# Mixer output projection: both groups normed before the product, summed in one PSUM bank

## The chip, the core and the metric

The kernel runs on one core of a Trainium2 chip. The metric is device time in microseconds of one execution. TensorE does the products, VectorE (DVE) and ScalarE (ACT) everything between them, SyncE (SP) issues the loads of weights.

## The reference, cut to what matters

Two transformer blocks on 512 tokens of width 1024, in fp32. The change touches the end of the first block's mixer and the start of its feed-forward part:

```python
a = mla(...)                      # 8 heads, 512 wide
c = short_gated_conv(...)         # 512 wide
m = jnp.concatenate([rmsnorm(a, attn_group_norm[i]),
                     rmsnorm(c, conv_group_norm[i])], axis=-1)
x = x + rmsnorm(m @ w_out[i], mix_post_norm[i])
h = rmsnorm(x, ffn_pre_norm[i])
...
e = rmsnorm(p[i] @ w_ple_proj[i], ple_norm[i])
```

Both group norms are over the 512 channels of a token, so their factor is one number per token. It can be applied to the operand of `m @ w_out` or to that group's product.

## The kernel before, in words

Activations lie channels by tokens, in tiles of 128 x 512. Every fp32 operand is split into a high and a low part (`split`: a copy on ACT, a subtraction on DVE), and a product of two 128-deep tiles is three matmuls (`mm3`, L170 to L172): this is called a unit here. Weights come as 128 x 1024 tiles through SP and are split as well (L131 on ACT, L115 on DVE), from three buffers each.

TensorE executes in the order in which the program is written (the schedule of that engine is manual, L82); ACT, DVE and SP are ordered by a planner that works from priorities and estimated times. The order on TensorE is written with Python generators that yield after each unit: `pull(gen, n)` puts n units at this place, `drain(gen)` the rest. `attention` (L557) runs eight heads; between a head's steps it pulls units from a fill, `per(h)` for head h, and `PER[2]` before the last head's product with the values.

A norm (`Norm`) has four steps. `square` adds up squares on ACT and DVE. `column` (L394) transposes the sums on TensorE and starts `root`, some ten small DVE instructions on one column, at raised priority. `spread` (L432) transposes the column back over 128 partitions on TensorE, and ACT copies the result to a tile `rb`. Then a tile is scaled with it (`apply_norm`, L148, DVE). `first()` queues what DVE is given meanwhile behind the root.

Before the change the group norms act on the products. `conv_out` (L824) multiplies the gated convolution's tiles, with only the gain applied (`split_gain`), by `w_oc`; each of 8 output tiles is scaled by `n_conv.r` on its way out of its bank into `ys`. `out_unit` (L893) does the same for the attention with `w_oa`: DVE scales the bank by `n_att.r` (L109), adds it to `ys` (L112), ACT squares the sum and DVE adds the square up for the norm that follows, `n_post`. The last three output tiles are done in two halves of 256 tokens, so that the first half's norm can start while the second half runs. `boundary` (L938) then goes on with the first half: its root beside units of the fill (`embed`, the projection of the layer's extra embedding), its spread, the residual sum, and the feed-forward part's first products, half by half.

The fill of the attention (`mixer_fill`, L836) holds, in this order: the projections of heads 1 to 6 and what is left of `w_in` (61 units in six shares), then the splits of the four convolution tiles, the projection of head 7, two of eight `embed` tiles, and `conv_out` with the column and the spread of its norm between its units. After the attention come six more units, the column of the attention's norm, the rest of the fill and four of the attention's units, then the spread.

Of the kernel before, what the change touches and what calls it, by code (L numbers as in the profile page):

```python
# [14 lines left out]
P = 128  # L15
T = 512
NT = T // P
D = 1024
KT = D // P
# [17 lines left out]
N_RET = (14, 6)  # L37
# [26 lines left out]
def kernel(  # L64
# [32 lines left out]
    def f32(ap):  # L97
        return ap.bitcast(F32)
# [31 lines left out]
    def copy(out, a):  # L130
        act.activation(out, a, AF.Copy)  # L131
# [37 lines left out]
    def mm3(out, ah, al, bh, bl, start, stop):  # L169
        pe.matmul(out, lhsT=ah, rhs=bh, start=start, stop=False)  # L170
        pe.matmul(out, lhsT=al, rhs=bh, start=False, stop=False)  # L171
        pe.matmul(out, lhsT=ah, rhs=bl, start=False, stop=stop)  # L172

    ALL = slice(0, T)
    HALVES = (slice(0, T // 2), slice(T // 2, T))

    def units(out, w, cols, acts, start=True, stop=True, tok=ALL):
        hi, lo = w  # L180
        n = len(acts)
        for i, (c, a) in enumerate(zip(cols, acts)):
            mm3(out[:, tok], hi[:, c:c + P], lo[:, c:c + P], a[:, 0, tok], a[:, 1, tok],
                start and i == 0, stop and i == n - 1)
            if i < n - 1:
                yield

    def load4(src, n, acts=None, prepare=None, start=0, pool=None):
# [429 lines left out]
    def embed(n):  # L618
        for mt in range(len(es), len(es) + n):
            if mt % 2 == 0:  # L620
                w = weights(w_ple_proj[(mt // 4) * P:(mt // 4 + 1) * P, mt % 4 * 2 * P:(mt % 4 + 2) * 2 * P], 4 * P)
            ps = bank()
            yield from units(ps, w, K8[:2] if mt % 2 == 0 else K8[2:4], pp)
            y = f32(es_t[mt // 2][:, mt % 2, :])
            with tc.high_priority(offset=HE):
                copy(y, ps)
            es.append(y)
            if mt >= 6:
                n_e.square(y)
            yield  # L630
# [4 lines left out]
    with tc.tile_pool(name="m1", bufs=1) as m1, tc.tile_pool(name="pt1", bufs=1) as ptp:  # L635
# [5 lines left out]
        hn = []  # L641
# [153 lines left out]
        qs = {}  # L795
        n_att, heads = Norm(512), []

        def split_head(i):
            heads.append(split_gain(att[i], g_("attn_gn", i)))
# [24 lines left out]
        def conv_out():  # L824

            for mt in range(KT):
                if mt % 2 == 0:
                    w = weights(rows(w_oc, mt // 2))
                    ys_t.append(pair())
                ps = bank()  # L830
                yield from units(ps, w, K8[mt % 2 * 4:mt % 2 * 4 + 4], mixed)
                ys.append(f32(ys_t[-1][:, mt % 2, :]))
                n_conv.then(lambda y=ys[-1], ps=ps: mul(y, ps, n_conv.r))
                yield

        def mixer_fill():  # L836
            for h in range(1, 7):
                yield from project(h)
                if h == 6:
                    embed_load()  # L840
                for _ in range(left * h // 6 - left * (h - 1) // 6):
                    next(fill, None)
                    yield
            yield from fill
            es_t.append(pair())
# [12 lines left out]
            n_conv.spread()  # L858
            yield from co

        def mla_head(h):
            def done(po):
                join(att[h // 2][64 * (h % 2):64 * (h % 2) + 64, :], po)
                if h % 2:
                    n_att.square(att[h // 2])
                    if h == 7:
                        split_head(3)
# [10 lines left out]
        for f in late:  # L878
# [1 line left out]
        pull(fill, LAT[5])  # L880
        left = 13 * KT - sum(LAT[:6])
        mf = mixer_fill()
        per = [left * (h + 1) // 6 - left * h // 6 + 2 + h % 2 * 2 for h in range(6)]
        attention(8, mla_head, mf, lambda h: per[h] if h < 6 else PER[h - 6], ptp, PER[2], urgent=True,
                  at_last=lambda: [split_head(i) for i in range(3)])
        pull(mf, OUT[0])
        n_att.column()
        with n_att.first():
            drain(mf)

        def out_unit(mt, ps, w, tok):  # L893
            yield from units(ps, w, K8[mt % 2 * 4:mt % 2 * 4 + 4], heads, tok=tok)

            def evacuate():
                y, t = ys[mt][:, tok], tmp()[:, tok]
                mul(t, ps[:, tok], n_att.r[:, tok])
                add(y, y, t)
                (n_post if tok == ALL else n_post.halves[HALVES.index(tok)]).square(y)  # L900
            n_att.then(evacuate)
            yield

        def att_out():
            for mt in range(5):
                if mt % 2 == 0:
                    w = weights(rows(w_oa, mt // 2))
                yield from out_unit(mt, bank(), w, ALL)

            ws = [w] + [weights(rows(w_oa, 3))] * 2  # L910
            ps3 = [bank() for _ in ws]
            n_post.fold()
            for tok in HALVES:
                for k in range(3):
                    yield from out_unit(5 + k, ps3[k], ws[k], tok)
# [40 lines left out]
        return banks, units4(banks, src, acts, loaded=loaded, tok=b.tok)  # L956


    es_t += [pair(), pair()]
# [616 lines left out]
```

## Time and profile before

| | |
|---|---|
| median of 3 runs | 1975.17 us (1974.32 to 1975.25) |
| profiled execution | 1974.2 us, its span 1972.5 us |
| TensorE busy | 1948.5 us, 99% of the span |
| DVE busy | 1289.7 us, 65% |
| ACT busy | 914.4 us, 46% |
| mean granted clock of TensorE | 0.996 of full |
| stretch of the change | about 140 to 252 us of the span |

The table is a sum over stages of different kinds. TensorE is busy nearly all the time, so what a change in one stage is worth shows in the few places where TensorE waits, and in the granted clock there.

### The profile page before, as it was taken

To read this page: it belongs to the slowest core of one execution; us is meant where nothing else is said; L and a number is where in the kernel's file an instruction comes from. 1 tells how busy PE (TensorE), PEld (TensorE's weight loads), DVE (VectorE), ACT (ScalarE), POOL (GpSimd) and SP (SyncE) were. 2 spreads that over 40 slices of the span, in tenths; PEclk is the share of its full clock that TensorE was granted. 3 is DMA by queue.
4 is the path that set the end of the run, shared out by engine and by line. 5 is a ranking of instruction groups with operands and counts; after the bars stand their busy time and mean duration, and the time that the engine had idled before them with its cause. 6 is when DMAs were issued, how large, how long until landed. Compare 5 with 4: busy or idle time off the path is not lost.

```text
span 1972.5 us, 26036 instructions
## 1 busy us (share of the span) xinstructions
PE 1948.5 (99%) x10212; PEld 1668.0 (85%) x10212; DVE 1289.7 (65%) x2322; ACT 914.4 (46%) x1557; POOL 9.7 (0%) x21
## 2 busy tenths in 40 slices
PE   9999999999999999999999999999999999999998
PEld 7787888888888888888888898898888888889897
DVE  7878963343459764636467575675598987667575
ACT  5776542232235444324445353444476755344352
POOL 1000000000000000000000000000000000000000
PEclk9999999999999999999999999999999999999999
DMA  5122223333232322232223332323322233332321
GB/s 186 65 65 91 86 85 96 97 97 96 91 118 75 108 80 80 97 96 75 75 92 103 105 97 96 118 86 99 91 88 83 74 102 107 97 116 88 118 75 65
DMA packets 59050, 185.44 MB, mean 94 GB/s; under 512 B 6928, under 2 KB 10400, under 8 KB 58928
## 3 DMA queue, kind: packets, MB, share of 16 engines
q1 hardware_dynamic: 53936, 176.02, 28.0%
q10 hardware_dynamic: 4688, 7.40, 1.2%
q8 instruction: 80, 1.31, 0.3%
q0 software_dynamic: 304, 0.36, 0.1%
q14 instruction: 42, 0.34, 0.1%
HBM read 181.56 MB, written 2.20 MB: 93 GB/s over the span
## 4 chain that ended last, share of the span: by engine, by line
PE 82%; DVE 10%; ACT 4%; DMA 2%; issue 2%; SPq 0%; POOLq 0%; POOL 0%; ACTq 0%; DVEq 0%
PE bank L172 25%; PE bank L170 25%; PE bank L171 24%; PE bank L311 6%; DVE pair L115 2%; DVE wl L115 2%; DMA qr<-in_m_w_dram 1%; ACT pair L131 1%; DVE tmp L112 1%; PE bank L532 1%; ACT wh L131 1%; PE bank L513 1%; ACT tmp L500 1%; DVE pt L115 1%; DVE tmp L1094 1%
## 5 line engine op out<-in xcount | busy, mean ns | idle before, releaser
L170 PE MATMUL bank<-pair,wh 128*128 128x512 f32 (+1 forms) x2166 | 829.7, 383 | 0.3 <-ACT pair L131 0.3
L172 PE MATMUL bank<-pair,wh 128*128 128x512 f32 (+1 forms) x2166 | 820.7, 379 | 0.5 <-DVE pair L115 0.3
L171 PE MATMUL bank<-pair,wl 128*128 128x512 f32 (+1 forms) x2166 | 819.3, 378 | 0.1
L131 ACT ACTIVATE wh<-wr 128x1024 fp32r<-128x1024 f32 (+5 forms) x331 | 326.1, 989 | 667.4 <-PE bank L172 404.2
L115 DVE TENSOR_TENSOR wl<-wr,wh 128x1024 fp32r<-128x1024 f32 (+5 forms) x331 | 375.7, 1138 | 159.5 <-ACT wh L131 158.5
L172 PEld LDWEIGHTS bank<-pair,wh 128*128 128x128 f32 x2166 | 408.0, 188 | 78.4 <-DVE pair L115 1.7
L171 PEld LDWEIGHTS bank<-pair,wl 128*128 128x128 f32 x2166 | 408.5, 189 | 72.4 <-DVE wl L115 0.9
L170 PEld LDWEIGHTS bank<-pair,wh 128*128 128x128 f32 x2166 | 408.5, 189 | 72.4 <-ACT pair L131 0.9
L131 ACT ACTIVATE pair<-tmp 128x512 fp32r<-128x512 f32 (+1 forms) x236 | 146.0, 627 | 86.2 <-DVE tmp L1313 25.9
L112 DVE TENSOR_TENSOR x<-x,bank 128x512 f32<-128x512 f32 (+1 forms) x99 | 66.0, 669 | 176.5 <-PE bank L172 176.4
L115 DVE TENSOR_TENSOR pair<-tmp,pair 128x512 fp32r<-128x512 f32 (+1 forms) x204 | 137.6, 686 | 17.7 <-ACT pair L131 16.0
L311 PE MATMUL bank<-q,pair 128*128 128x256 f32 x1152 | 146.3, 282 | 1.2 <-DVE bank L112 1.1
L311 PEld LDWEIGHTS bank<-q,pair 128*128 128x128 f32 x1152 | 140.7, 189 | 3.7 <-DVE bank L112 3.7
L109 DVE TENSOR_TENSOR tmp<-bank,rb 128x512 f32<-128x512 f32 (+1 forms) x76 | 50.2, 666 | 103.9 <-PE bank L172 101.6
L1095 ACT ACTIVATE tmp<-tmp 128x512 f32<-128x512 f32 x64 | 40.2, 629 | 89.0 <-DVE tmp L1094 89.0
L170 PE MATMUL bank<-wh,pair 128*128 128x512 f32 x200 | 79.3, 396 | 0.6 <-ACT tmp L131 0.6
L172 PE MATMUL bank<-wl,pair 128*128 128x512 f32 x200 | 78.0, 390 | 0.0
L171 PE MATMUL bank<-wh,pair 128*128 128x512 f32 x200 | 77.9, 389 | 0.0
L311 PE MATMUL bank<-pair,wh 128*128 128x256 f32 x384 | 76.3, 282 | 0.0
L500 ACT ACTIVATE tmp<-tmp,small 128x512 f32<-128x512 f32 (+1 forms) x96 | 53.4, 557 | 33.4 <-DVE small L497 32.2
L112 DVE TENSOR_TENSOR tmp<-tmp 128x512 f32<-128x512 f32 (+1 forms) x90 | 56.8, 632 | 14.0 <-ACT tmp L385 13.4
L311 PEld LDWEIGHTS bank<-pair,wh 128*128 128x128 f32 x384 | 62.5, 189 | 0.2
(182 smaller groups left out, 1846.4 us busy)
## 6 DMA issues: line engine op xcount, KB each, us to landing
wr<-in_m_w_dram SPq DMA_DIRECT2D x104, 512.0 KB, 3.7
wr<-in_r_qkg_dram SPq DMA_DIRECT2D x32, 512.0 KB, 3.5
qr<-in_m_w_dram SPq DMA_DIRECT2D x24, 512.0 KB, 3.7
wr<-in_w_gate_dram SPq DMA_DIRECT2D x20, 512.0 KB, 3.5
wr<-in_w_up_dram SPq DMA_DIRECT2D x20, 512.0 KB, 3.5
wr<-in_w_down_dram SPq DMA_DIRECT2D x16, 512.0 KB, 3.4
wr<-in_r_v_dram SPq DMA_DIRECT2D x16, 512.0 KB, 3.5
wr<-in_r_out_dram SPq DMA_DIRECT2D x16, 512.0 KB, 3.7
```

The source lines that it names most:

```text
L109: dve.tensor_tensor(out=out, in0=a, in1=b, op=ALU.mult)
L112: dve.tensor_tensor(out=out, in0=a, in1=b, op=ALU.add)
L115: return dve.tensor_tensor(out=out, in0=a, in1=b, op=ALU.subtract)
L131: act.activation(out, a, AF.Copy)
L170: pe.matmul(out, lhsT=ah, rhs=bh, start=start, stop=False)
L171: pe.matmul(out, lhsT=al, rhs=bh, start=False, stop=False)
L172: pe.matmul(out, lhsT=ah, rhs=bl, start=False, stop=stop)
L311: pe.matmul(out, lhsT=x[:, c], rhs=y, start=start and k + i == 0, stop=k == 3 and i == 2, skip_group_check=True)
L500: act.activation(s[:, :n], s[:, :n], AF.Exp, bias=self.mx[:, col], scale=-1.0, accum_out=self.sm[:, col])
L513: pe.transpose(pt[:, j * P:(j + 1) * P], s[:, j * P:(j + 1) * P], ident)
L532: pe.matmul(o, lhsT=a, rhs=b, start=j == 0 and a is v, stop=j == NT - 1 and a is v)
L1095: act.activation(t, t, AF.Square)
```

## The change

Both groups are normed before their products: `normed` applies the factor and the gain on DVE and splits the result. The convolution's products then stay in their banks (`out_ps`) and the attention's products add up on top of them (`start=False`). A bank is copied out by ACT and squared from the bank by ACT (`evacuate`). The first three output tiles are done row by row of the operand (`by_rows`), for the convolution and for the attention, so that one normed tile serves three banks. Seven banks are held from the convolution's products on; the eighth output tile's convolution products are done in halves just ahead of its attention products. The norm of the convolution gets its column and its spread between four `embed` tiles; the shares of the fill are spread over seven heads and not six.

```diff
-W_OUT = (8, 3, 5, 13, 13)
+W_OUT = (8, 2, 2, 13, 13)
-PER = (14, 10, 6)
-OUT = (6, 6)
+PER = (10, 6)
+OUT = 6
-CO = (4, 11)
+CO = (4, 4)
+    def by_rows(outs, ws, cols, acts, start):
+        for k, a in enumerate(acts):
+            for out, w, c in zip(outs, ws, cols):
+                c = slice(c + k * P, c + k * P + P)
+                mm3(out, w[0][:, c], w[1][:, c], a[:, 0, :], a[:, 1, :], start and k == 0,
+                    k == len(acts) - 1, True)
+                yield
+        def normed(norm, src, gname, i):
+            t, pr = tmp(), pair()
+            apply_norm(t, src, g_(gname, i), norm.r)
+            split(pr, t)
+            return pr
         def conv_out():
-            for mt in range(KT):
...
-                n_conv.then(lambda y=ys[-1], ps=ps: mul(y, ps, n_conv.r))
+            ws = [weights(rows(w_oc, i)) for i in range(2)]
+            out_ps.extend(bank() for _ in range(3))
+            yield from by_rows(out_ps, (ws[0], ws[0], ws[1]), (0, T, 0), mixed, True)
+            for mt in range(3, 7):
...
         def mixer_fill():
-            for h in range(1, 7):
+            for h in range(1, 8):
...
-            for c in range(4):
-                mixed.append(split_gain(conv[c], g_("conv_gn", c)))
-            yield from project(7)
-            yield from embed(2)
-            co = conv_out()
+            em = embed(4)
             for _ in range(CO[0]):
-                next(co)
+                next(em)
                 yield
             n_conv.column()
             for _ in range(CO[1]):
-                next(co)
+                next(em, None)
                 yield
             n_conv.spread()
-            yield from co
+            for c in range(4):
+                mixed.append(normed(n_conv, conv[c], "conv_gn", c))
+            yield from em
+            yield from conv_out()
...
-        pull(mf, OUT[0])
+        pull(mf, OUT)
         n_att.column()
         with n_att.first():
             drain(mf)
+        n_att.spread()
+        for i in range(4):
+            heads.append(normed(n_att, att[i], "attn_gn", i))
+        def evacuate(mt, tok):
...
+            copy(ys[mt][:, tok], out_ps[mt][:, tok])
+            (n_post if tok == ALL else n_post.halves[HALVES.index(tok)]).square(out_ps[mt][:, tok])
         def att_out():
+            ws = [weights(rows(w_oa, i)) for i in range(2)]
+            yield from by_rows(out_ps[:3], (ws[0], ws[0], ws[1]), (0, T, 0), heads, False)
+            for mt in range(3):
+                evacuate(mt, ALL)
...
         out = att_out()
-        with n_att.first():
-            pull(out, OUT[1])
-        n_att.spread()
-        pull(out, 32 + W_OUT[0] - OUT[1])
+        pull(out, 36 + W_OUT[0])
         n_post.halves[0].column()
...
-    banks, rest = boundary(n_post, ys, "mix_post", ffn_in, embed(4), W_OUT, w_gu, hn, w4)
+    banks, rest = boundary(n_post, ys, "mix_post", ffn_in, embed(2), W_OUT, w_gu, hn, w4)
```

## Rows read from the trace of the kernel before

**Rows 1.** The page, busy time by engine: us, share of the span, instructions.
```profile
PE 1948.5 (99%) x10212; PEld 1668.0 (85%) x10212; DVE 1289.7 (65%) x2322; ACT 914.4 (46%) x1557; POOL 9.7 (0%) x21
```
**Rows 2.** Waits of TensorE, 140 to 340 us: us in total, times, longest.
```profile
PE bank L398 <- DVE tmp L112: 3.3, 2, 2.3
...
PE bank L435 <- DVE small L423: 0.8, 1, 0.8
```
**Rows 3.** Timeline, last heads: start, us, engine line, xcount [idle before <-releaser].
```profile
152.27 0.63 ACT L131 ACTIVATE pair<-tmp 128x512 fp32r<-128x512 f32 x1 [0.61 <-DMA tmp<-in_pT_dram]
...
153.40 0.51 PE L532 MATMUL bank<-pt,pair 128*128 128x512 f32 x1 [0.90 <-ACT pt L131]
...
154.44 1.20 PE L532 MATMUL bank<-pt,pair 128*64 128x512 f32 x7 [0.54 <-DVE pt L115]
...
168.98 0.62 PE L513 MATMUL bank<-ident,tmp 128*128 128x128 f32 x3 [1.56 <-ACT tmp L504]
```
**Rows 4.** Windows: busy PE, PEld, DVE, ACT, POOL, granted clock, DMA share, GB/s.
```profile
152.00:156.00 4.00, 2.57 (x13) 1.78 (x12) 4.00 (x9) 3.73 (x8) 0.00 (x0) 0.97 0.35 113
156.00:160.00 4.00, 4.00 (x15) 3.40 (x15) 3.12 (x7) 3.86 (x8) 0.00 (x0) 0.61 0.07 23
168.00:172.00 4.00, 3.02 (x15) 2.54 (x16) 3.71 (x16) 1.77 (x5) 0.00 (x0) 1.00 0.25 63
214.00:218.00 4.00, 1.66 (x11) 1.47 (x10) 3.85 (x12) 0.84 (x2) 0.00 (x0) 0.90 0.67 207
218.00:222.00 4.00, 4.00 (x17) 3.25 (x16) 2.78 (x12) 2.05 (x4) 0.00 (x0) 0.68 0.15 57
```
**Rows 5.** Windows by stage: head 6 with its neighbours, and the attention's output products.
```profile
153.00:169.00 16.00, 13.51 (x62) 10.85 (x62) 14.33 (x35) 14.30 (x30) 0.00 (x0) 0.89 0.31 99
197.00:217.00 20.00, 17.66 (x110) 15.78 (x109) 17.65 (x33) 9.29 (x17) 0.00 (x0) 1.00 0.32 109
```
**Rows 6.** Timeline from the attention norm's column to the first half's column.
```profile
190.81 0.66 PE L398 MATMUL bank<-ident,tmp 128*128 128x128 f32 x4
...
195.71 0.16 DVE L423 SCALAR_TENSOR_TENSOR small<-small 128x4 f32<-128x4 f32 x1
...
196.77 0.60 PE L435 MATMUL bank<-ident,small 128*128 128x128 f32 x4
...
197.13 0.48 PE L170 MATMUL bank<-pair,wh 128*128 128x512 f32 x1
...
199.96 0.39 PE L170 MATMUL bank<-pair,wh 128*128 128x512 f32 x1
...
200.64 0.39 PE L170 MATMUL bank<-pair,wh 128*128 128x512 f32 x1
...
212.95 0.28 PE L170 MATMUL bank<-pair,wh 128*128 128x256 f32 x1
...
213.31 0.28 PE L170 MATMUL bank<-pair,wh 128*128 128x256 f32 x1
...
216.53 0.44 PE L398 MATMUL bank<-ident,tmp 128*128 128x128 f32 x2 [2.34 <-DVE tmp L112]
```
**Rows 7.** Timeline of the latents' norm: its spread, and the first tile's split.
```profile
51.22 1.09 PE L435 MATMUL bank<-ident,small 128*128 128x128 f32 x8 [0.74 <-DVE small L423]
...
53.32 0.63 ACT L131 ACTIVATE pair<-tmp 128x512 fp32r<-128x512 f32 x1 [0.33 <-DVE tmp L148]
...
54.53 0.69 DVE L115 TENSOR_TENSOR pair<-tmp,pair 128x512 fp32r<-128x512 f32 x1
```
**Rows 8.** Timeline of the convolution's norm: its column and the end of its root.
```profile
163.27 0.60 PE L398 MATMUL bank<-ident,tmp 128*128 128x128 f32 x4
...
171.95 0.15 DVE L109 TENSOR_TENSOR small<-small 128x4 f32<-128x4 f32 x1
```
**Rows 9.** Groups by shape, 197 to 217 us: xcount, busy, mean ns, idle before.
```profile
L109 DVE TENSOR_TENSOR tmp<-bank,rb 128x512 f32<-128x512 f32 x5 | 3.4, 688 | 2.3 <-ACT rb L131 1.6 <-PE bank L172 0.7
```
**Rows 10.** Timeline: ACT copies an embedding tile out of its bank.
```profile
221.38 0.60 ACT L131 ACTIVATE pair<-bank 128x512 f32<-128x512 f32 x1 [0.60 <-PE bank L172]
```

More of the change, by code (lines that the diff above doesn't have):

```diff
@@ L167, in rows, with mm3, units @@
         return src[mt * P:(mt + 1) * P, k0 * P:(k0 + nk) * P]
[L169 to L172, printed above, removed]
+    def mm3(out, ah, al, bh, bl, start, stop, loose=False):
+        pe.matmul(out, lhsT=ah, rhs=bh, start=start, stop=False, skip_group_check=loose)
+        pe.matmul(out, lhsT=al, rhs=bh, start=False, stop=False, skip_group_check=loose)
+        pe.matmul(out, lhsT=ah, rhs=bl, start=False, stop=stop, skip_group_check=loose)
     ALL = slice(0, T)
     HALVES = (slice(0, T // 2), slice(T // 2, T))
-    def units(out, w, cols, acts, start=True, stop=True, tok=ALL):
+    def units(out, w, cols, acts, start=True, stop=True, tok=ALL, loose=False):
         hi, lo = w
@@ L183, in units @@
             mm3(out[:, tok], hi[:, c:c + P], lo[:, c:c + P], a[:, 0, tok], a[:, 1, tok],
-                start and i == 0, stop and i == n - 1)
+                start and i == 0, stop and i == n - 1, loose)
             if i < n - 1:
+                yield
[5 more added lines that the diff above has]
+                    k == len(acts) - 1, True)
                 yield
@@ L796 @@
         n_att, heads = Norm(512), []
-        def split_head(i):
-            heads.append(split_gain(att[i], g_("attn_gn", i)))
         def project(h):
@@ L822, in project @@
             yield
-        def conv_out():
-            for mt in range(KT):
[L827 to L832, printed above, removed]
-                n_conv.then(lambda y=ys[-1], ps=ps: mul(y, ps, n_conv.r))
+        def normed(norm, src, gname, i):
[3 more added lines that the diff above has]
+            return pr
+        out_ps = []
+        def conv_out():
+            ws = [weights(rows(w_oc, i)) for i in range(2)]
+            out_ps.extend(bank() for _ in range(3))
+            yield from by_rows(out_ps, (ws[0], ws[0], ws[1]), (0, T, 0), mixed, True)
+            for mt in range(3, 7):
+                if mt == 3:
+                    w = ws[1]
+                elif mt % 2 == 0:
+                    w = weights(rows(w_oc, mt // 2), 8 * P if mt < 6 else 4 * P)
+                out_ps.append(bank())
+                yield from units(out_ps[-1], w, K8[mt % 2 * 4:mt % 2 * 4 + 4], mixed, loose=True)
                 yield
         def mixer_fill():
-            for h in range(1, 7):
+            for h in range(1, 8):
                 yield from project(h)
@@ L840, in mixer_fill @@
                     embed_load()
-                for _ in range(left * h // 6 - left * (h - 1) // 6):
+                for _ in range(left * h // 7 - left * (h - 1) // 7):
                     next(fill, None)
@@ L844, in mixer_fill @@
             yield from fill
-            es_t.append(pair())
-            for c in range(4):
-                mixed.append(split_gain(conv[c], g_("conv_gn", c)))
-            yield from project(7)
-            yield from embed(2)
-            co = conv_out()
+            es_t.extend(pair() for _ in range(2))
+            em = embed(4)
             for _ in range(CO[0]):
-                next(co)
+                next(em)
                 yield
@@ L882 @@
         mf = mixer_fill()
-        per = [left * (h + 1) // 6 - left * h // 6 + 2 + h % 2 * 2 for h in range(6)]
-        attention(8, mla_head, mf, lambda h: per[h] if h < 6 else PER[h - 6], ptp, PER[2], urgent=True,
-                  at_last=lambda: [split_head(i) for i in range(3)])
-        pull(mf, OUT[0])
+        per = [left * (h + 1) // 7 - left * h // 7 + 2 + h % 2 * 2 for h in range(7)] + [PER[0]]
+        attention(8, mla_head, mf, lambda h: per[h], ptp, PER[1], urgent=True)
+        pull(mf, OUT)
         n_att.column()
@@ L889 @@
             drain(mf)
[L893 to L902, printed above, removed]
-        def att_out():
[L905 to L908, printed above, removed]
+        n_att.spread()
@@ new lines @@
+        for i in range(4):
+            heads.append(normed(n_att, att[i], "attn_gn", i))
+        def evacuate(mt, tok):
+            if len(ys) == mt:
+                if mt % 2 == 0:
+                    ys_t.append(pair())
+                ys.append(f32(ys_t[-1][:, mt % 2, :]))
+            copy(ys[mt][:, tok], out_ps[mt][:, tok])
+            (n_post if tok == ALL else n_post.halves[HALVES.index(tok)]).square(out_ps[mt][:, tok])
+        def att_out():
+            ws = [weights(rows(w_oa, i)) for i in range(2)]
+            yield from by_rows(out_ps[:3], (ws[0], ws[0], ws[1]), (0, T, 0), heads, False)
+            for mt in range(3):
+                evacuate(mt, ALL)
+            w = ws[1]
+            for mt in (3, 4):
+                if mt == 4:
+                    w = weights(rows(w_oa, 2))
+                yield from units(out_ps[mt], w, K8[mt % 2 * 4:mt % 2 * 4 + 4], heads, start=False, loose=True)
+                evacuate(mt, ALL)
+                yield
@@ L910, in att_out @@
             ws = [w] + [weights(rows(w_oa, 3))] * 2
-            ps3 = [bank() for _ in ws]
+            last = weights(w_oc[3 * P:4 * P, 4 * P:8 * P], 4 * P)
+            out_ps.append(bank())
             n_post.fold()
             for tok in HALVES:
-                for k in range(3):
-                    yield from out_unit(5 + k, ps3[k], ws[k], tok)
+                for mt in (5, 6, 7):
+                    c = K8[mt % 2 * 4:mt % 2 * 4 + 4]
+                    if mt == 7:
+                        yield from units(out_ps[mt], last, K8[:4], mixed, tok=tok, loose=True)
+                        yield
+                    yield from units(out_ps[mt], ws[mt - 5], c, heads, start=False, tok=tok, loose=True)
+                    evacuate(mt, tok)
+                    yield
@@ L956, in boundary @@
         return banks, units4(banks, src, acts, loaded=loaded, tok=b.tok)
-    es_t += [pair(), pair()]
+    es_t.append(pair())
     hn = [pair() for _ in range(KT)]
```

2 lines of the change are left out of this document (removed).

## The prediction

> **What bounds the kernel now.** I read the page first: TensorE is busy 99% of the span, DVE 65% [rows 1]. Only two things can move the time: how much TensorE has to do, and where it waits or runs slow. So next come the waits of TensorE in the stretch of the change, 140 to 340 us. The reader is to see that they are few: 3.3 us in two transposes of norm sums, one of them 2.3, and 0.8 for a spread [rows 2]; the timeline of the last heads adds 0.90 and 0.54 before a product with the values and 1.56 before a transpose [rows 3]. Third, the granted clock around each. After the 0.90 and 0.54 the mean clock is 0.97 and then 0.61 of two windows of 4 us; after the 2.34 it is 0.90 and 0.68; after the 1.56 it stays 1.00 [rows 3, 4, 6]. The missing clock is (0.03 + 0.39) x 4 = 1.68 us and (0.10 + 0.32) x 4 = 1.68 us: TensorE at 1.2 and not 2.4 GHz for about twice as long. A wait can so cost its length, or 1.68 us more. Last, the load by stage: between 197 and 217 us DVE is busy 17.65 of 20 us, ACT 9.29; in 153 to 169 both about 14.3 of 16 [rows 5]. All waits and lost clock of this stretch sum to 0.90 + 0.54 + 1.56 + 3.3 + 0.8 + 2 x 1.68 = 10.5 us. No gain can be much larger.
>
> **TensorE's own work.** The products are the same. Only the eighth output tile's 12 convolution matmuls become 24 of half width. A unit of three takes 200.64 - 199.96 = 0.68 us at 512 columns and 213.31 - 212.95 = 0.36 at 256 [rows 6]: 8 x 0.36 - 4 x 0.68 = +0.15 us. Two embed tiles move ahead, out of the boundary. SP issues one load more for the same bytes, since the last quarter of `w_oc` is fetched as two halves; weights wait for buffers and not for the bytes, so nothing.
>
> **The convolution's norm.** I count the yields of the new fill. Projections and `w_in` give 20 + 61 = 81, which is just what heads 0 to 6 pull. So head 7's ten pulls are eight embed units and two of `conv_out`. The column stands after the fourth embed unit, the spread after the eighth, and behind the spread comes the first convolution unit, with nothing between: four embed tiles are eight units, so `yield from em` is empty by then. Two waits follow. First the root. Its cover is the column's own transposes (197.13 - 196.77 = 0.36 us for four [rows 6]), four units of 0.68 and the turn's four transposes: 3.45 us. The attention norm's root took 195.87 - 190.81 = 5.06 us from the first transpose [rows 6], the convolution's, which has four instructions more and shared DVE with a head, 172.10 - 163.27 = 8.8 [rows 8]. That bounds the wait at 5.06 - 3.45 = 1.6 and 5.4; a DVE with an empty queue could bring it to 0. I take 1.6, since the heavy splits of the convolution tiles no longer stand beside it. Behind the wait stand the turns of head 7, which need the same engine. Second, spread to first product: ACT copies `rb`, DVE applies, ACT makes the high part. The latents' norm runs this very chain: from the spread at 51.22 to the end of the high part at 53.95 is 2.73 us, to the end of the low part 55.22 [rows 7]. Five units lie between there; here none. Less the four transposes it is 2.73 - 0.36 = 2.4 us; the third matmul needs the low part, 0.69 us behind the high and 0.46 after the first: +0.2. Together 2.6; upper bound 55.22 - 51.22 - 0.36 - 0.46 = 3.2. A clock fall follows a wait of such a length (2.34 had one, 1.56 none): 1.7, bounds 0 and 1.7. Sum 1.6 + 2.6 + 1.7 = +5.9, from 2.4 to 10.3.
>
> **The attention's norm.** Of the fill's 81 + 8 + 28 = 117 units 103 are pulled when the column stands; 14 remain, 14 x 0.68 = 9.5 us against a root of 5.06 [rows 6]: covered twice. But `drain` puts all 14 ahead of the spread, and behind the spread comes the first attention unit. The chain of 2.6 us is bare again; the bounds are 2.4 and 3.2, and above that the split of a weight tile whose buffer comes free just then. After it the rows hold: one normed tile costs DVE 2 x 0.69 us and serves three units, 2.05. With the clock, 2.6 + 1.7 = +4.3, from 2.4 to 6. Before, six units of the attention were free of the factor and stood there, with no wait at 196.77 [rows 6].
>
> **The evacuation.** Before, each attention tile costs DVE a scale (five full ones, 688 ns each [rows 9]), a sum like it and the square's sum; now it costs ACT a copy (0.60 us from a bank [rows 10]) and a square, and DVE the last alone. Five full tiles save DVE 5 x 2 x 0.69 = 6.9 us and the halves more, in a stage where it is the fuller engine [rows 5]. What is late at 216.53 is DVE's sum of squares, and eight half units (2.9 us) cover it in both kernels. Now the queue behind the last half tile is a copy and a square on ACT and one sum on DVE, under 1.5 us. The wait of 2.34 and its lost clock go: -4.0, bounds -4.0 and 0.
>
> A rule speaks against it. Before, each output product had a bank that DVE left soon; at 212.95 the second halves go into the banks of the first halves without a wait [rows 6]. The Trainium skill's Perfetto Trace Analysis, section Matmuls, says that independent groups should rotate through different PSUM banks, so that the evacuation of one lies beside the next one's products. Here three banks end together and seven are held. By the rule TensorE would wait for ACT at the second halves; by the row it doesn't, and the sum stays.
>
> **The last heads.** The four convolution splits leave the stage where ACT and DVE are fullest [rows 5], and the `w_oc` splits move one head on: the 1.56 goes (-1.6, bounds -1.6 and 0). The 0.90 and 0.54 stand behind ACT, which waited for an input of the embedding before it could make the next `pt` [rows 3]; that load stays where it was in the fill: 0, bounds -3.1 (with its clock) and 0. Twelve units fewer, 8.2 us, lie between the same steps of the softmax. DVE and ACT have room in the earlier heads, where the trace shows no wait: 0, bound +3.1, the price of one more stall like that of rows 3.
>
> **The boundary.** Two embed units, 1.36 us, and not five stand between the first half's spread and its first product. The chain is that of rows 7 on half tiles, without the `rb` copy: I take +0.4, from 0 to 2.73 - 1.36 = 1.4. Ahead of the spread stand eight half units and two full ones, 4.2 us, against a root of 5.06 on a full DVE: 0, bound +0.9.
>
> **Sum.** 0.15 + 5.9 + 4.3 - 4.0 - 1.6 + 0.4 = +5.2 us on an execution of 1974.2 us; the median of the runs lies 1.0 above it at 1975.17, so 1980.4.
>
> **Rivals.** (1) Not slower: relief of ACT and DVE in the last heads. It decides if the convolution's root is done by the spread, that is if DVE is empty enough to finish within 3.45 us. Then 1.6 goes, its clock holds as it did after 1.56 (1.7), and the same relief frees the `pt` copies, so that 0.90, 0.54 and their clock go (3.1): 5.2 - 6.4 = -1.2, 1974.0. If the second new wait keeps its clock too and the 0.97 and 0.8 left in rows 2 go, -1.2 - 1.7 - 1.8 = -4.7, 1970.5. For it: the 1.56 without a fall, and the splits' departure. Against: in rows 8 the root took 8.8. (2) ACT becomes the bound of the evacuation, as the rule above has it. Five tiles at 2 x 0.60 us, three halves at about 0.8 and some 4 us of weight splits come to an estimated 12 us, in the 8 x 0.68 + 24 x 0.36 = 14 us between the end of the first three tiles and the column. If the planner puts the splits first, the 4.0 isn't won: +9.2, 1984.4. For it: as little spare. Against: ACT has half its time free there [rows 5]. (3) The heads, thinner by 12 units, wait once more, clock included: 5.2 + 3.1, 1983.5. For it: 14.3 of 16 us [rows 5]; against: no wait in heads 0 to 4. (4) That the change doesn't do what it says: its products do run beside the attention's root, but not beside the steps behind the spread; that is my forecast.
>
> **Numbers.** Forecast 0.42 (its own range 1977.5 to 1984), rival 1 0.28, rival 2 0.14, rival 3 0.16. A measurement tells 0.2% from no change, 3.95 us. The forecast gives slower 0.30, same 0.12; rival 1 faster 0.11, same 0.17; the others slower 0.23, same 0.07. Range for 8 in 10: 1972.5 (rival 1 without all its parts) to 1985.5 (rival 2 and a little).
>
> **What would show it.** Right: in the waits, L170 or the like waiting for ACT's high part twice, over 2 us each, behind the two spreads (L435); a low clock after each; no wait at the first half's column. Wrong: no wait behind a spread, which would say that I misread the order; a wait at L398 on the square's sum (rival 2); waits at L513 or L532 in heads 0 to 5 (rival 3). The forecast falls if the clock holds after both new waits.

## The result, and the profile after

The changed kernel takes 1984.9 us (median of 5 runs, 1984.0 to 1985.9) against 1974.3 of the kernel before in the same rounds: ratio 1.0054 [1.0043, 1.0065], slower by 10.6 us. The forecast was slower by 5.2. The profiled span is 1984.1 us against 1972.5. From the start of the latents' spread to that of the norm that follows the feed-forward part's sum, the stage that the change touches, it is 216.85 us against 206.73: 10.1 of the 11.6 lie there.

Busy time by engine on the page of the kernel after, which answers to [rows 1]:

```profile
PE 1951.8 (98%) x10224; PEld 1669.5 (84%) x10224; DVE 1280.8 (65%) x2301; ACT 918.7 (46%) x1569; POOL 9.7 (0%) x21
```

The twelve more matmuls are the eighth tile's halves; DVE gave up 9 us, ACT took 4. TensorE is busy for 3.3 us longer, about half of it the low clock read below; the other 7 us are waits. TensorE's waits from 60 to 270 us of the kernel after (us in total, times, longest):

```profile
PE bank L171 <- ACT pair L131: 5.4, 2, 3.3
PE bank L523 <- ACT tmp L514: 2.8, 4, 1.2
PE bank L445 <- DVE small L109: 2.6, 1, 2.6
PE bank L171 <- ACT pair L142: 2.0, 1, 2.0
PE bank L408 <- DVE tmp L112: 0.9, 1, 0.9
PE bank L171 <- ACT tmp L131: 0.6, 1, 0.6
PE bank L173 <- DVE pair L115: 0.5, 1, 0.5
```

They sum to 14.8 us; before it was 7.7 ([rows 2, 3] and one of 0.6 that both kernels have). The old ones but that and the 0.9 are gone. The new ones stand at the two spreads that the change put bare in TensorE's order (with no independent product behind them), at the turns of the thinner heads (the transposes of a head's softmax, L523) and at the boundary.

The convolution's norm in the timeline of the kernel after (start, us, engine line, xcount, [idle before <- releaser]):

```profile
165.60 0.60 PE L408 MATMUL bank<-ident,tmp 128*128 128x128 f32 x4
...
167.07 1.05 ACT L131 ACTIVATE wh<-wr 128x1024 fp32r<-128x1024 f32 x1
...
168.16 1.23 DVE L115 TENSOR_TENSOR wl<-wr,wh 128x1024 fp32r<-128x1024 f32 x1 [0.57 <-ACT wh L131]
...
169.30 0.16 DVE L109 TENSOR_TENSOR small<-small 128x4 f32<-128x4 f32 x1
...
171.97 0.65 PE L445 MATMUL bank<-ident,small 128*128 128x128 f32 x4 [2.58 <-DVE small L109]
...
172.65 0.60 ACT L131 ACTIVATE rb<-bank 128x512 f32<-128x512 f32 x1 [0.57 <-PE bank L445]
...
174.07 1.95 ACT L131 ACTIVATE pair<-tmp 128x512 fp32r<-128x512 f32 x3 [0.82 <-DVE tmp L148]
...
174.75 0.80 PE L171 MATMUL bank<-pair,wh 128*128 128x512 f32 x1 [2.14 <-ACT pair L131]
```

Two waits, as forecast: 2.58 us for the root and 2.14 for the chain copy, scale, high part. The row at 168.16 says why the root was late: DVE stood 0.57 us for ACT and then split a weight tile for 1.23, between the root's first instructions and the rest. The attention's norm:

```profile
189.68 0.60 PE L408 MATMUL bank<-ident,tmp 128*128 128x128 f32 x4
...
192.43 0.16 DVE L433 SCALAR_TENSOR_TENSOR small<-small 128x4 f32<-128x4 f32 x1
...
199.67 0.60 PE L445 MATMUL bank<-ident,small 128*128 128x128 f32 x4
...
199.87 1.06 ACT L131 ACTIVATE wh<-wr 128x1024 fp32r<-128x1024 f32 x1 [1.66 <-PE bank L173]
...
200.94 0.60 ACT L131 ACTIVATE rb<-bank 128x512 f32<-128x512 f32 x1
200.95 1.22 DVE L115 TENSOR_TENSOR wl<-wr,wh 128x1024 fp32r<-128x1024 f32 x1 [1.49 <-ACT wh L131]
202.10 2.07 DVE L148 SCALAR_TENSOR_TENSOR tmp<-att,gn,rb 128x512 f32<-128x512 f32 x3
...
203.56 0.50 PE L171 MATMUL bank<-pair,wh 128*128 128x512 f32 x1 [3.29 <-ACT pair L131]
```

The root is done at 192.59; fourteen units stand ahead of the spread all the same, which runs 7.1 us later, and behind it TensorE has nothing. ACT begins a weight's split just before the spread ends, so `rb` comes 0.67 us after the spread's last transpose; DVE then makes that weight's low part, so the scale starts at 202.10, 0.56 us after `rb` is done.

The windows of the kernel after around these two places, over the attention's products, and around the boundary (busy time of PE, PEld, DVE, ACT, POOL, then granted clock, DMA share, GB/s):

```profile
172.00:176.00 4.00, 1.83 (x6) 0.87 (x6) 3.89 (x6) 2.54 (x5) 0.00 (x0) 0.81 0.48 135
176.00:180.00 4.00, 3.99 (x12) 3.24 (x13) 2.78 (x6) 1.32 (x5) 0.00 (x0) 0.50 0.05 19
180.00:184.00 4.00, 4.00 (x16) 3.23 (x15) 0.92 (x3) 0.26 (x1) 0.00 (x0) 0.84 0.00 0
...
204.00:208.00 4.00, 3.47 (x10) 2.56 (x9) 3.30 (x7) 2.13 (x5) 0.00 (x0) 0.65 0.23 87
208.00:212.00 4.00, 4.00 (x17) 3.20 (x17) 1.23 (x3) 0.34 (x1) 0.00 (x0) 0.93 0.22 68
...
200.00:228.00 28.00, 24.18 (x133) 20.75 (x132) 16.28 (x25) 16.83 (x33) 0.00 (x0) 0.94 0.34 114
...
234.00:238.00 4.00, 1.89 (x12) 1.26 (x11) 4.00 (x11) 2.45 (x5) 0.00 (x0) 1.00 0.73 245
238.00:242.00 4.00, 4.00 (x36) 4.00 (x35) 3.95 (x11) 2.05 (x5) 0.00 (x0) 1.00 0.02 4
```

The missing clock behind the convolution's waits is (0.19 + 0.50 + 0.16) x 4 = 3.4 us, 1.2 GHz for 6.8 us; behind the attention's (0.35 + 0.07) x 4 = 1.7. DVE and ACT now share the evacuation about evenly (16.28 and 16.83 of 28 us; in [rows 5] it was 17.65 and 9.29 of 20). Head 0's turns, the first half's column, a weight's split on DVE behind the boundary's spread and the first product after it, in the timeline:

```profile
81.42 0.44 PE L523 MATMUL bank<-ident,tmp 128*128 128x128 f32 x2 [0.54 <-ACT tmp L514]
...
83.03 0.33 PE L523 MATMUL bank<-ident,tmp 128*128 128x128 f32 x1 [1.18 <-ACT tmp L514]
...
228.34 0.38 PE L408 MATMUL bank<-ident,tmp 128*128 128x128 f32 x2
...
233.26 1.23 DVE L115 TENSOR_TENSOR wl<-wr,wh 128x1024 fp32r<-128x1024 f32 x1 [0.52 <-ACT wh L131]
...
236.59 0.39 PE L171 MATMUL bank<-pair,wh 128*128 128x256 f32 x1 [2.03 <-ACT pair L142]
```

At 228.34 the 2.34 us of [rows 6] are gone, and the clock holds. At 81 to 83 and at 236.59 there are waits that the kernel before did not have.

### The profile page after: what moved, and what is told of

Same layout as the page of the kernel before. It is cut to its first block, busy times and chain, and to the rows that moved or that the text cites. A ratio compares the mean times of both kernels' runs of the same rounds, so it can differ in the third digit from the quotient of the medians.

```text
span 1984.1 us, 26050 instructions
## 1 busy us (share of the span) xinstructions
PE 1951.8 (98%) x10224; PEld 1669.5 (84%) x10224; DVE 1280.8 (65%) x2301; ACT 918.7 (46%) x1569; POOL 9.7 (0%) x21
## 3 DMA queue, kind: packets, MB, share of 16 engines
q1 hardware_dynamic: 54080, 176.02, 27.8%
## 4 chain that ended last, share of the span: by engine, by line
PE 80%; DVE 11%; ACT 6%; issue 2%; DMA 1%; POOLq 0%; POOL 0%; DVEq 0%; ACTq 0%
PE bank L173 24%; PE bank L171 24%; PE bank L172 24%; PE bank L321 5%; DVE pair L115 2%; DVE wl L115 2%; ACT pair L131 1%; DMA qr<-in_m_w_dram 1%; ACT wh L131 1%; DVE tmp L112 1%; ACT tmp L510 1%; PE bank L542 1%; PE bank L523 1%; DVE pt L115 1%; ACT tmp L131 1%
## 5 line engine op out<-in xcount | busy, mean ns | idle before, releaser
L131 ACT ACTIVATE pair<-tmp 128x512 fp32r<-128x512 f32 (+1 forms) x244 | 151.0, 627 | 87.4 <-DVE tmp L1336 26.2
L115 DVE TENSOR_TENSOR pair<-tmp,pair 128x512 fp32r<-128x512 f32 (+1 forms) x212 | 142.7, 686 | 18.7 <-ACT pair L131 16.9
L109 DVE TENSOR_TENSOR tmp<-bank,rb 128x512 f32<-128x512 f32 x65 | 44.3, 688 | 101.2 <-PE bank L173 100.9
L112 DVE TENSOR_TENSOR tmp<-tmp 128x512 f32<-128x512 f32 (+1 forms) x90 | 56.9, 633 | 15.9 <-ACT tmp L395 15.4
```

Of the source, the lines that this page charges most:

```text
L115: return dve.tensor_tensor(out=out, in0=a, in1=b, op=ALU.subtract)
```

## The experiments

The theory: the time went into chains between engines that lie bare behind a spread, and into the low clock behind them. Rivals: ACT as the evacuator is the bound; the thinner heads are; the waits matter little beside the clock. Each diff is against the changed kernel; times are medians of four to eleven runs, ratios are against the kernel before.

**e1: units behind the attention's spread.** Seven of the fourteen units of the fill stand ahead of the spread and seven behind it.

```diff
-            drain(mf)
+            pull(mf, 7)
         n_att.spread()
         for i in range(4):
             heads.append(normed(n_att, att[i], "attn_gn", i))
+        drain(mf)
```

> The changed kernel, with 7 of the 14 convolution units moved behind the spread of the attention's norm; 7 stay between its column and the spread. Theory (the chain behind the spread is bare): 7 units are 4.8 us, the chain took 3.3 + 0.5, so both waits go, and the low clock of 3.4 us behind them with its 1.7: 5.5 us less than the changed kernel, +5.1 over the kernel before; the root, 2.8 us from column to end, still fits the 4.8 ahead of the spread. Rival (ScalarE and VectorE bound this stage, so that a covered wait comes back at a later product): the waits of TensorE between 185 and 230 us sum to about 3 as they did, and the time stays within 2 us of the changed kernel's +10.6.

Measured: 1981.6 us, ratio 1.0038 [1.0025, 1.0051]. In the timeline of e1 the chain is there as before, and no wait of TensorE in it:

```profile
194.81 0.60 PE L445 MATMUL bank<-ident,small 128*128 128x128 f32 x4
...
195.45 0.60 ACT L131 ACTIVATE rb<-bank 128x512 f32<-128x512 f32 x1 [2.77 <-PE bank L445]
```

Both attention waits (3.29 and 0.53) and the low clock behind them are gone; 5.5 us together. The clock fell elsewhere, behind the boundary's wait, which is as long as in the changed kernel, where the clock held. The windows of e1 there:

```profile
228.00:232.00 4.00, 1.89 (x12) 1.26 (x11) 4.00 (x11) 2.52 (x5) 0.00 (x0) 1.00 0.74 251
232.00:236.00 4.00, 4.00 (x23) 4.00 (x23) 3.88 (x11) 2.05 (x5) 0.00 (x0) 0.57 0.01 4
```

That costs 0.43 x 4 = 1.7, so that 3.8 us should be left; the stage is 4.65 shorter (212.20), 0.8 more than I can place. What follows: the attention's 5.5 us are the bare chain and the clock behind it, and seven units hide it. The intervals of the two ratios overlap, so it is the trace and not the times that shows it.

**e2: the convolution's spread behind one embed unit.** The column after the first of eight embed units, the spread after the fifth, so that three units lie behind it.

```diff
-CO = (4, 4)
+CO = (1, 4)
```

> The changed kernel, with the column of the convolution's norm after the first embed unit and its spread after the fifth (CO = (1, 4)), so that three embed units and a turn stand behind the spread. Theory: the root of 6.3 us has 5.4 us of work beside it and not 3.5, so its wait falls from 2.6 to about 0.7; the chain of 2.6 has 2.4 us of work, so its wait falls from 2.1 to 0.2; the double fall of the clock (6.8 us, 3.4 lost) doesn't come: 7 us less than the changed kernel, +3.5 over the kernel before. Rival (head 7 is short of ScalarE and VectorE, not of cover): the waits turn up at the turns of head 7 or at the product with its values, 3 us or more, and the gain is under 3 us.

Measured: 1986.5 us, 1.0059 [1.0046, 1.0073]. No gain. In the timeline of e2:

```profile
164.05 0.66 PE L408 MATMUL bank<-ident,tmp 128*128 128x128 f32 x4 [1.61 <-DVE tmp L112]
...
169.90 0.62 PE L445 MATMUL bank<-ident,small 128*128 128x128 f32 x4
170.35 1.05 ACT L131 ACTIVATE wh<-wr 128x1024 fp32r<-128x1024 f32 x1
...
172.62 1.06 ACT L131 ACTIVATE wh<-wr 128x1024 fp32r<-128x1024 f32 x1
...
174.35 2.18 ACT L131 ACTIVATE pair<-tmp 128x512 fp32r<-128x512 f32 x4
...
175.02 0.50 PE L171 MATMUL bank<-pair,wh 128*128 128x512 f32 x1 [2.00 <-ACT pair L131]
```

The root is covered now, but the column waits 1.61 us for the sum of squares, and the chain behind the spread takes 169.90 to 174.95, 5.0 us and not 2.7: the planner put a weight's split ahead of `rb` and another, with two pieces of head 7's softmax (0.39 and 0.57 us on ACT), ahead of the high part. My theory was incomplete: the chain has no fixed length. What stands ahead of it in the queues of ACT and DVE sets it. The waits of this norm so sum to 4.5 us against 4.7. The clock behind them is low for 3.4 us and not 6.8, but it fell anew in two places that the edit doesn't touch, behind head 0's turns and behind the boundary's wait, for 3.4 us each, which loses 1.7 twice. Without these two e2 would be an estimated 2 us faster than the kernel after (1.7 of clock and 0.2 of waits), not the 7 expected.

**e3: the waits filled with idle products.** Products into a spare bank that nobody reads (512 columns each), so that TensorE is busy where it waited; they add work that the kernel doesn't need.

```diff
+        def busy(n):
+            ps = bank()
+            for _ in range(n):
+                pe.matmul(ps, lhsT=pp[0][:, 0, :P], rhs=pp[0][:, 0, :], start=True, stop=True)
...
+            busy(10)
             n_conv.spread()
+            busy(8)
...
         n_att.spread()
+        busy(8)
```

> The changed kernel with matmuls of 512 columns whose result nobody reads: 10 ahead of the convolution norm's spread, 8 behind it, 8 behind the attention norm's spread. They fill about 2.3, 1.8 and 1.8 us of the three waits and shorten no chain. If the low clock follows the waits and costs what the windows say, the falls at 174 and 205 us go and with them 3.4 + 1.7 = 5.1 us, while wait and filler together stay as long: +5.5 over the kernel before. If the falls cost nothing or don't follow the waits, the time stays at +10.6; if the fillers delay the products, it rises above.

Measured: 1983.5 us, 1.0048 [1.0035, 1.0060], not told apart from the changed kernel. Both falls are gone; the first window is behind the convolution's spread, where the kernel after has 0.81. But one came behind head 0's turns, whose waits are as before (second window). Both of e3:

```profile
172.00:176.00 4.00, 3.46 (x17) 2.25 (x15) 3.72 (x9) 2.58 (x6) 0.00 (x0) 1.00 0.44 128
...
82.00:86.00 4.00, 3.19 (x9) 2.52 (x10) 3.94 (x8) 2.56 (x6) 0.00 (x0) 0.63 0.25 28
```

At the attention's spread 1.33 us of wait are left ahead of the idle products. They lengthen nothing: from the convolution's column to its first product it is 9.17 us (166.85 to 176.02) where the kernel after has 9.15, from the attention's spread to its first product 3.90 (198.51 to 202.41) and 3.89. The stage is 2.5 us shorter: 5.1 of low clock gone, 1.7 new in head 0, and 0.5 for the convolution's third matmul, which at the full clock waits for its low part (0.53 at 177.28); 0.4 stay open. So the two falls belong to the two waits. The Trainium skill's TensorE: Matmul & The Clock Gate, section HAM oscillation, tells alike of another kernel, where each wait for a DMA, of about 3 to 5 us, was followed by the lower clock and half of the low stretch was lost: here it is half as well, 3.4 of 6.8 us, but not every wait has a fall behind it (the boundary's 2.03 us has none).

**e4: DVE evacuates.** The banks are scaled by DVE into a temporary tile and summed, so that ACT has only the square, as in the kernel before.

```diff
-            copy(ys[mt][:, tok], out_ps[mt][:, tok])
+            y, t = ys[mt][:, tok], tmp()[:, tok]
+            dve.tensor_scalar(t, out_ps[mt][:, tok], 0.5, None, ALU.mult)
+            add(y, t, t)
...
-            (n_post if tok == ALL else n_post.halves[HALVES.index(tok)]).square(out_ps[mt][:, tok])
+            (n_post if tok == ALL else n_post.halves[HALVES.index(tok)]).square(y)
```

> The changed kernel, but each bank leaves through VectorE as before the change: half of it to a temporary tile, the sum of that with itself to the result, and ScalarE squares the result. VectorE has two instructions a tile more, ScalarE one less. Theory (the gain of 4.0 at the first half's column came from taking these two off VectorE): a wait of 2 us or more at that column comes back, with a low clock: 3 to 4 us more than the changed kernel, about +14 over the kernel before. Rival (that wait went because TensorE now arrives later, VectorE having caught up during the wait behind the attention's spread): no wait there, and the time stays within 1 us of +10.6.

Measured: 1992.2 us, 1.0090 [1.0077, 1.0104]; 7.3 us more than the changed kernel. In the timeline of e4:

```profile
227.44 0.38 PE L171 MATMUL bank<-pair,wh 128*128 128x256 f32 x1 [0.42 <-DVE tmp L913]
...
229.65 0.38 PE L171 MATMUL bank<-pair,wh 128*128 128x256 f32 x1 [0.52 <-DVE tmp L913]
...
233.06 0.44 PE L408 MATMUL bank<-ident,tmp 128*128 128x128 f32 x2 [1.72 <-DVE tmp L112]
```

The wait at the first half's column is back with DVE's queue, 1.72 us, and the second halves wait 0.42 and 0.52 for a bank that DVE still reads. The Trainium skill's Perfetto Trace Analysis, section Matmuls, whose rule the prediction weighs, wants independent groups to rotate through different PSUM banks, so that the evacuation of one overlaps the next one's products. The trace agrees where the evacuator is late, as here; in the kernel after, with ACT, no second half waits. The low clock that I had expected behind the column's wait didn't come; one came in head 0, which the edit doesn't touch. With its 1.7 the stage is 4.8 us longer; some 2.5 us of the 7.3 lie elsewhere, unexplained.

**e5: embed units behind the boundary's spread.** Both of the first pull's units are moved there.

```diff
-W_OUT = (8, 2, 2, 13, 13)
+W_OUT = (8, 0, 4, 13, 13)
```

> The changed kernel with all four embed units of the boundary behind the first half's spread and none ahead of it (W_OUT = (8, 0, 4, 13, 13)). Theory (cover): the wait of 2.0 us at the feed-forward part's first product falls by 2 x 0.68 to about 0.7, and the root, 2.8 us from column to end, has 8 half units, 2.9 us, beside it: 1.4 us less than the changed kernel, +9.2 over the kernel before, or 3 less where a fall of the clock followed that wait. Rival (VectorE's queue sets that product, not the spread): the wait stays and the time with it.

Measured: 1984.7 us, 1.0054 [1.0040, 1.0068]. The 2.03 us behind the first half's spread are gone; 0.6 came at the second half's, as in [rows 2]. The convolution's waits are as in the changed kernel, 2.6 and 2.1, but behind them the clock is low for 3.4 us and not 6.8. All waits from 60 to 270 us are 1.8 us fewer (0.5 of them at the attention's third matmul), the clock gives 1.7, and the stage is 3.1 shorter; the run times, which scatter over 4 us, don't show it.

**e6: more units for head 0.** Shares of 10, 9, 9, 9, 9, 8, 7 in place of about equal ones.

```diff
+SHARE = [10, 9, 9, 9, 9, 8, 7]
...
-                for _ in range(left * h // 7 - left * (h - 1) // 7):
+                for _ in range(SHARE[h - 1]):
...
-        per = [left * (h + 1) // 7 - left * h // 7 + 2 + h % 2 * 2 for h in range(7)] + [PER[0]]
+        per = [SHARE[h] + 2 + h % 2 * 2 for h in range(7)] + [PER[0]]
```

> The changed kernel with shares of the fill of 10, 9, 9, 9, 9, 8, 7 units for heads 0 to 6 in place of 8, 9, 9, 8, 9, 9, 9: head 0 pulls 12 units and not 10, as before the change. Theory (thin heads wait for their softmax): the waits of head 0 at its last turns, 0.54 + 1.18, go, and now and then a low clock behind them; 1.7 us less, +8.9. Rival (head 0 is late for its own reason, such as the convolution's gates on VectorE): they stay, and head 6 with 9 units and not 11 gets a new wait.

Measured: 1987.4 us, 1.0062 [1.0049, 1.0076]. Head 0's waits are gone, and new ones stand in later heads, of which the timeline of e6 has:

```profile
124.94 1.20 PE L543 MATMUL bank<-pt,pair 128*64 128x512 f32 x7 [1.26 <-DVE pt L116]
...
157.59 0.55 PE L524 MATMUL bank<-ident,tmp 128*128 128x128 f32 x3 [1.76 <-ACT tmp L515]
```

At the turns and before the values together 4.5 us against 2.8. Head 6, which gave two units, waits 3.2 at its turns (0.7 in the kernel after); that fits heads that lack units in all, so that moving them moves the wait. The 1.26 in head 3, which got a unit, doesn't follow from its share and stays open.

**e7: the convolution normed by a ratio.** The convolution's operand gets the gain alone, ready long before; the attention's gets its factor over the convolution's; the sum is scaled by the convolution's factor on its way out, by DVE.

```diff
+            for c in range(4):
+                mixed.append(split_gain(conv[c], g_("conv_gn", c)))
             em = embed(4)
...
             n_conv.column()
+            inv.append(...)
+            dve.reciprocal(inv[0], n_conv.col)
...
             n_conv.spread()
-            for c in range(4):
-                mixed.append(normed(n_conv, conv[c], "conv_gn", c))
...
         n_att.column()
+        mul(n_att.col, n_att.col, inv[0])
...
-            copy(ys[mt][:, tok], out_ps[mt][:, tok])
+            mul(ys[mt][:, tok], out_ps[mt][:, tok], n_conv.r[:, tok])
...
```

> The changed kernel, but the convolution's products no longer wait for their norm: the gain alone is applied ahead of them, the attention's column is divided by the convolution's (two small VectorE instructions), and each bank is multiplied by the convolution's factor as VectorE takes it out, in place of ScalarE's copy; the sum is the same. Theory (the convolution's root of 2.6, its chain of 2.1 and the double low clock of 3.4 stand in the path only since its products need the factor): all three go, 8 us less than the changed kernel, and VectorE's extra 0.69 a tile costs at most 1 us at the first half's column: about +3 over the kernel before. Rival (heads 6 and 7 are short of ScalarE and VectorE, as they were before the change): the convolution's splits back in head 7 make waits of 3 us or more at its turns, and the gain is under 4.

Measured: 1982.1 us, 1.0038 [1.0025, 1.0052]. The waits of e7 in place of the kernel after's 5.4 and 2.6:

```profile
PE bank L171 <- ACT pair L131: 3.3, 1, 3.3
...
PE bank L445 <- DVE small L109: 2.9, 1, 2.9
```

The 2.14 us of the chain are gone, the root's wait stayed; 2.8 us are won and not 8. I had overlooked that the spread itself stands in TensorE's order and waits for the root, whoever uses what it spreads. Behind the convolution's wait the clock is low for 3.4 us, behind the attention's now for 6.8. The banks now leave through DVE, in one instruction a tile, and no wait stands at the first half's column: so e4's wait points to the two instructions a tile there, not to DVE as such.

**e8: e7 with e1, e5 and e6.**

```diff
 # e7, and
-W_OUT = (8, 2, 2, 13, 13)
+W_OUT = (8, 0, 4, 13, 13)
+SHARE = [10, 9, 9, 9, 9, 8, 7]
...
+            pull(mf, 7)
         n_att.spread()
...
+        drain(mf)
```

> The four edits together: the ratio of e7, 7 convolution units behind the attention's spread, the boundary's embed units behind its spread, and the shares of e6. If the waits add up as the theory has them, the stage keeps only what the change saves: -8.1 - 5.5 - 1.4 - 1.7 from +10.6, that is about -6 against the kernel before, 1968. If a covered wait comes back elsewhere (rival), it ends between -2 and +5.

Measured: 1978.7 us, 1.0017 [1.0008, 1.0026]. Of the convolution's root 1.3 us of wait are left and 1.3 at spreads of the halves, but 4.3 at the turns and 1.3 before the values, with 6.8 us of low clock from 160.6 on. The heads are now the largest part, and the 6 us below the kernel before that I expected didn't come.

**e9: e7 with e1 and e5, and the convolution's spread behind twelve of its units.** Shares as in the changed kernel.

```diff
 # e7, with pull(mf, 7) and drain(mf) as in e1, W_OUT as in e5, and
-            n_conv.spread()
             yield from em
-            yield from conv_out()
+            co = conv_out()
+            for _ in range(12):
+                next(co)
+                yield
+            n_conv.spread()
+            yield from co
```

> The changed kernel with the ratio of e7, the spread of the convolution's norm moved behind the first twelve convolution units (its result is needed only when the banks are emptied), 7 convolution units behind the attention's spread as in e1, and all boundary embed units behind the first half's spread as in e5; the shares stay as changed. Theory: nothing in the path waits for the convolution's norm any more, so its root wait (2.6 in the changed kernel, 2.9 in e7) goes too; what is left in 60 to 270 us are the thin heads' 2.8 and about 1.5 at later columns, with one fall of the clock or none: 10.6 - 2.6 - 2.1 - 3.4 - 5.5 - 2.0 = -5 against the kernel before, 1970. Rival (a covered wait comes back at the next product that ScalarE or VectorE feeds): waits of 3 us or more at the turns of heads 6 and 7 as in e8, and a time at or above the kernel before.

Measured: 1973.1 us, 0.9989 [0.9980, 0.9998]. No wait at either norm, no low clock in the stage; left are 4.1 us at the turns (1.9 of them new, in head 7), 1.3 at spreads of the halves, 0.8 and 0.6. Against the kernel after that is 8 us of waits and 5.1 of low clock less, 13.1 together; the stage (51.32 to 255.41) is 12.8 us shorter.

**e10: e9 with four more units between the steps of the heads.** Of the fourteen that stood behind the attention's column ten are left, five ahead of the spread and five behind it.

```diff
 # e9, and
-        attention(8, mla_head, mf, lambda h: per[h], ...
+        attention(8, mla_head, mf, lambda h: per[h] + (2, 0, 0, 0, 1, 0, 1, 0)[h], ...
...
-            pull(mf, 7)
+            pull(mf, 5)
```

> e9 with two more pulls in head 0, one in head 4 and one in head 6, which brings later units forward, and 5 and 5 of the remaining convolution units on either side of the attention's spread. Theory (thin heads wait): the waits at the last turns of heads 0, 4 and 6, 2.8 together, fall to under 1, and five units, 3.4 us, still cover the root of 2.8 and all but 0.5 of the chain: 1.5 less than e9. Rival (as e6 showed, a unit given to one head is missed at another): the sum of waits at turns and at the products with the values stays at 2.8 or more, and the time is that of e9 or above.

Measured: 1970.2 us (1969.7 to 1971.9), 0.9975 [0.9965, 0.9985]: 4.7 us faster than the kernel before. Its waits from 60 to 270 us, and the window over them all, whose clock is 1.00:

```profile
PE bank L445 <- DVE small L433: 2.0, 2, 1.0
PE bank L408 <- DVE tmp L112: 1.0, 2, 0.8
PE bank L171 <- ACT tmp L131: 0.6, 1, 0.6
...
60.00:267.00 207.00, 202.85 (x1117) 172.80 (x1116) 172.26 (x396) 142.03 (x288) 0.00 (x0) 1.00 0.25 77
```

With 0.2 at a turn and 0.2 before values they sum to 4.0 us, against 14.8 in the changed kernel and 7.7 before. The stage is 200.94 us, 5.8 shorter than before and 15.9 shorter than in the kernel after; 10.8 us of waits and 5.1 of low clock are 15.9 too. So with the norms' chains hidden the change can be part of a faster kernel. What the one bank alone is worth isn't shown: the kernel before, with waits of its own in the last heads, wasn't given other units there.

## Why the prediction was right, and where its sizes were off

Forecast and measured by the terms of the sum (waits from the timelines, clock from the windows):

| term | forecast | measured |
|---|---|---|
| TensorE's own work | +0.15 | +0.15 taken, not read by itself |
| convolution's norm | 1.6 + 2.6 + 1.7 = +5.9 | 2.58 + 2.14 + 3.4 = +8.1 |
| attention's norm | 2.6 + 1.7 = +4.3 | 3.29 + 0.53 + 1.7 = +5.5 |
| evacuation | -4.0 | -4.0 |
| heads | -1.6 | -1.56 - 0.90 - 0.54 - 1.7 + 2.8 = -1.9 |
| boundary | +0.4 | 2.0 - 0.8 = +1.2; -0.1 at the second half's column |
| sum | +5.2 | +8.95 |

The stage grew by 10.1; about 1.1 us of it are in no wait or window that I read. They don't come from the new waits: e10 has 3.7 us of waits and 3.4 of low clock less than the kernel before, 7.1 together, and a stage only 5.8 shorter. So they may belong to TensorE's own work in its new order; the cause stays open. The rest of the kernel differs by 1.5 us between the two profiles, and by up to 3.1 among the profiles of all these kernels. The mechanism was right, in place and order: both waits stand behind the two spreads, the first behind its root as well, the clock falls after both, and the evacuation's wait is gone. The number was right with some luck: 1984.9 lies 4.5 above the forecast of 1980.4 and above the forecast's own range (to 1984), and the stated range held it because it reached to 1985.5 for rival 2, which didn't come. Sizes were off:

- **Convolution's norm, the clock**, +1.7: I gave one low stretch of the length in [rows 4]; behind two waits with 0.65 us of transposes between them it lasted twice as long. It has either length behind about the same waits (6.8 in the kernel after, 3.4 in e5).
- **Convolution's norm, the root**, 2.58 for 1.6. I took the heavy splits to be gone from beside it; but a weight tile of `w_oc` itself was split there, and DVE's queue waits in order. The attention's root, with nothing beside it, took 2.9 us (189.68 to 192.59); with the convolution's four more instructions, 0.2 us apart, that is an estimated 3.7 against 3.45 of cover, a wait of 0.3. The chain itself took the 2.7 us of [rows 7]; it came out as a wait of 2.14 and not 2.6 because its four transposes, with no product behind them, took 0.65 of it and not 0.36, and because at the low clock the third matmul found its low part ready.
- **Attention's norm, the chain**, 3.82 for 2.6. I had named the split of a weight tile ahead of it as what could lengthen it, and took none; it was there, 1.06 us on ACT ahead of `rb` and 1.22 on DVE ahead of the scale.
- **Heads**: the net was nearly right for wrong reasons. The 0.90, the 0.54 and the low clock, kept at 0, went (3.1), and heads 0, 4 and 6 wait 2.8 anew (the sign of rival 3, which I priced at 3.1, though no low clock came with it). e10, where four more units between the steps bring 4.1 us at the turns down to 0.2, shows that it is units that the heads lack.
- **Boundary**: 2.03, where the bound behind the spread was 1.4; the first product waits for ACT's scaled high part (L142). I took the chain of [rows 7], but DVE split a weight tile here (233.26, 1.23 us) ahead of the scale, and the residual sum stands between the scale and the high part. e5, with two more units there, has no such wait.

Of the rivals, the relief of DVE (1) fell: the root wasn't done in time. ACT as the bound (2) fell at 228.34, and e4 shows the old evacuation, two instructions on DVE a tile, as the worse one.

## What to carry to other kernels

A factor applied ahead of a product puts a chain over three engines into TensorE's order: keep independent units for behind the spread, not only for the root ahead of it. Count that cover against the chain with the weight splits that the planner may queue ahead of it: from the spread to the end of the first high part it took 2.7 us with none, 3.8 with one (in the kernel after) and 5.0 with two and some softmax work (in e2). A factor common to a sum can be divided out and applied at the end, so that one group needs no factor before its product.

## What the runs showed of the hardware

The same wait is not always followed by a low clock. The boundary's 2.03 us stand in the kernel after, e3, e6 and e7 with the clock at 1.00, and in e1 (0.57) and e2 with a fall; head 0's 0.54 and 1.18 us had a fall in e2, e3 (0.63) and e4, and none in the kernel after, e1, e5, e7 and e9. The low stretches that I read took about 3.4 or 6.8 us. So, by these runs, a forecast of the clock behind a wait of about 2 us is good to 1.7 us a place and no better.
